# Hybrid decoder block: x loaded as rows, scaled and turned by TensorE, in place of x^T with sums over partitions

## The chip, the cores and the metric

One core of a Trainium2 chip runs the whole block as one launch. The metric is the device time in microseconds; three runs of the kernel before gave 1325.47, 1326.5 and 1329.25, median 1326.5. The engines named below are TensorE (PE; PEld is its weight load), VectorE (DVE), ScalarE (ACT), GpSimd (POOL) and the sync engine (SP), which issues nearly all loads.

## The reference

x is 1024 tokens by 1024 features, all float32. What the change touches is the first line of the block and the first product behind it:

```python
mod = silu(c) @ w_ada + b_ada            # six rows of 1024: shift_mix, scale_mix, gate_mix, ...
y   = x * rsqrt(mean(x * x, axis=-1) + 1e-6) * g_mix
h   = y * (1 + scale_mix) + shift_mix
qkv = h @ w_in                           # 1024 x 3072: q, k, v of 8 dilated and 8 stick-breaking heads
```

Then come the dilated ALiBi attention and the stick-breaking attention (64 wide heads), their RMS norms, the output projection with a gated residual, a second modulated RMS norm, a router (best of 4 groups, best 2 of its 8 experts), 32 SwiGLU experts of width 512, and a final RMS norm.

## The kernel before

**Layout.** The projection keeps features on the partitions: `hh[k]` and `hl[k]` (k = 0 to 7) are the high and the low part of h^T, each 128 features by 1024 tokens. A product in float32 is made of three passes in the faster float32r type: high weights by `hh`, low weights by `hh`, high weights by `hl`. For that the host hands x in two layouts: rows (`x`, used later for the residual) and turned (`xT`). All 128x1024 float32 tiles share one pool of 49 buffers (`slot`, L129), four PSUM banks are shared by `bank`, two double banks by `wide`.

**Loads.** SP issues them in program order: `c`, then `xT` as 16 pieces of 128x512 (first all eight k of tokens 0 to 511, then of 512 to 1023; L195 to L197), `cols` (biases and gains), `ident`, and the 20 loads of `LOADS0` (L51), 512 KB each: `10` is the 128x1024 block of w_ada^T that gives scale_mix for k = 0, `00` the one for shift_mix, `w0` and `w1` the weights of q and k of the first head pair, `w2` and `w3` those of v.

**The head (L249 to L312).** For each half of the tokens, ScalarE squares eight 128x512 tiles and VectorE adds them up (`add_sq`). The sum over the partitions is made by TensorE, four matmuls with a column of ones (`sums`); an inverse root by Newton steps (`rsqrt`, 12 small instructions for four columns on VectorE) gives 1/rms per token as a column, on GpSimd for the first half. `over_rows` brings it along the free axis: ident scaled by the roots, then a matmul with ones, so that PSUM holds 1/rms of each token on all partitions (`Rps`), copied to `Rb`. `w0_split(i)` makes the high part of a weight tile on ScalarE and the low part on the engine that `LO` names.

**The loop over k (L1074 to L1117).** `mod_k(k)` (L241) makes the gain `amix` and the shift of feature block k: two 128x1024 multiply-and-reduce instructions on VectorE (`ada_red`, L208, its line is L209) and two small ones. k = 0 is done in halves from `Rps` directly. For k from 1, GpSimd (VectorE for k = 1) multiplies `xT[k]` by `Rb`; ScalarE makes `hh[k] = gain * xT + shift` (L1093), ScalarE or VectorE makes the same in float32 (`tmp`), and VectorE takes the difference `hl[k]` (L1099, L1103). Each k then feeds 12 matmuls of 512 columns (L1119 to L1121, q and k of the first pair) and 15 of 256 columns (`v_first`, L1065, five of the eight token tiles). After the loop 72 matmuls of 256 columns make the other three token tiles. Each engine takes its instructions in program order, so a wait holds all behind it.

**Behind it.** The results are split into high and low parts, and the attention starts (L513 is its first VectorE step). All later stages are queued behind the earlier ones on each engine; the loads of the expert weights (L982) are tied to ScalarE instructions of the stage in which they are issued and to free buffers.

Of the kernel before, what the change touches and what calls it, by code (L numbers as in the profile page):

```python
# [7 lines left out]
F32 = mybir.dt.float32  # L8
# [4 lines left out]
AF = mybir.ActivationFunctionType  # L13
ALU = mybir.AluOpType
# [5 lines left out]
D = 1024  # L20
KT = 8
# [20 lines left out]
LDS = [6, 6, 11, 14, 18, 22, 28, 33, 33, 34]  # L42
PACE = 14
TZ, DZ = 2, 3
W2 = [0, 0]
W3 = [2, 3]
SK = 7
WT = 8
TM = "VVAAAAAA"
P2 = 2  # L50
LOADS0 = "10 w0 00 w1 11 01 w2 12 02 13 03 w3 14 04 15 05 16 06 17 07"  # L51
LO = 'GGGV'
M1 = "V"
VP = 5
VE = 'AVVAAVVV'
UT = 1
# [39 lines left out]
def build(nc, tc, I, out, cap=CAP):  # L96
# [6 lines left out]
    cp = pool("const", 1)  # L103
# [7 lines left out]
    E_ = dict(S=nc.sync, A=A, G=G, V=V)  # L111
# [26 lines left out]
    def f32(ap):  # L138
        return ap.bitcast(F32)
# [51 lines left out]
    crow = slot("crow")  # L191
    nc.sync.dma_start(crow[0:1], I["c"])
    halves = (slice(0, 512), slice(512, 1024))
    xT = [slot(f"xT{k}") for k in range(KT)]
    for c in halves:  # L195
        for k in range(KT):
            nc.sync.dma_start(xT[k][:, c], I["xT"][k * 128:(k + 1) * 128, c])  # L197
    nc.sync.dma_start(cols, I["cols"])
    nc.sync.dma_start(ident, I["ident"])
    sc = slot("sc")  # L200
# [7 lines left out]
    def ada_red(w, v, k):  # L208
        V.tensor_tensor_reduce(w, w, sc, op0=ALU.mult, op1=ALU.add, scale=1.0, scalar=0.0,  # L209
                               accum_out=modc[:, v * 8 + k:v * 8 + k + 1])  # L210
# [17 lines left out]
            v, k = int(o[0]), int(o[1])  # L228
            wa[v, k] = ada(v, k)

    def gain(k):
        ada_red(wa[1, k], 1, k)
        V.tensor_add(mod3[:, 1, k:k + 1], mod3[:, 1, k:k + 1], bad3[:, 1, k:k + 1])
        V.scalar_tensor_tensor(amix[:, k:k + 1], modc[:, 8 + k:9 + k], 1.0, g_mix[:, k:k + 1],
                               op0=ALU.add, op1=ALU.mult)

    def shift(k):
        ada_red(wa[0, k], 0, k)
        V.tensor_add(mod3[:, 0, k:k + 1], mod3[:, 0, k:k + 1], bad3[:, 0, k:k + 1])

    def mod_k(k):  # L241
        ada_red(wa[1, k], 1, k)
        ada_red(wa[0, k], 0, k)
# [6 lines left out]
    for c in halves:  # L250
        PE.matmul(cps[:, c], ones[0:1, :], crow[0:1, c], start=True, stop=True)
    A.activation(sc[:, 0:1], eps, AF.Silu)
    sq = [slot(f"xsq{k}") for k in range(KT)]
    rx = cp.tile([128, KT], F32, name="rx")
    dgs = slot("dgs")
    Rps = {}
    def warm(n):

        if n:
            scr = bank("scr")  # L260
            for _ in range(n * 4):
                PE.matmul(scr[:, 0:128], onesb, onesb, start=True, stop=True)

    def add_sq(h, ks):
        c = halves[h]
        for k in ks:
            A.activation(sq[k][:, c], xT[k][:, c], AF.Square)
            if k:
                V.tensor_add(sq[0][:, c], sq[0][:, c], sq[k][:, c])

    def sums(h):
        ssx = bank(f"ssx{h}", (128, 4))
        for tt in range(4):
            j = 4 * h + tt
            PE.matmul(ssx[:, tt:tt + 1], sq[0][:, j * 128:(j + 1) * 128], ones[:, 0:1], start=True, stop=True)
        warm(W2[h])
        return ssx

    def over_rows(h, eng):
        Rps[h] = bank(f"Rps{h}")  # L280
        for tt in range(4 * h, 4 * h + 4):
            dg = dgs[:, tt * 128:(tt + 1) * 128]
            if eng is A or tt % 2:
                A.activation(dg, ident, AF.Copy, scale=rx[:, tt:tt + 1])
            else:
                V.tensor_scalar_mul(dg, ident, rx[:, tt:tt + 1])
            PE.matmul(Rps[h][:, (tt - 4 * h) * 128:(tt - 4 * h + 1) * 128], ones, dg, start=True, stop=True)
        warm(W3[h])

    add_sq(0, range(KT))  # L290
    ss0 = cp.tile([128, 4], F32, name="ss0")
    ps = sums(0)
    add_sq(1, range(SK))
    A.activation(ss0, ps, AF.Copy)
    rsqrt(rx[:, 0:4], ss0, 4, 1.0 / D, G)
    add_sq(1, range(SK, KT))
    A.activation(sc, cps, AF.Silu)
    ss1 = sums(1)
    over_rows(0, A)
    wsp = {}  # L300

    def w0_split(i):
# [2 lines left out]
        E_[LO[i]].tensor_sub(lo, wraw[i], f32(hi))  # L305
        wsp[i] = [w.rearrange("p (k c) -> p k c", k=KT if i < 2 else 4) for w in (hi, lo)]

    Rb = slot("Rb")
    gain(0)
    w0_split(0)  # L310
    rsqrt(rx[:, 4:8], ss1, 4, 1.0 / D)
    over_rows(1, V)  # L312

    hh, hl = [], []
    pw = [wide("pj0"), wide("pj1")]
# [758 lines left out]
    for k in range(KT):  # L1074
        a = slot(f"hh{k}", F32R)
        b = slot(f"hl{k}", F32R)
        am, sh = amix[:, k:k + 1], modc[:, k:k + 1]
        if k == 0:
            c0, c1 = halves
            V.scalar_tensor_tensor(xT[k][:, c0], xT[k][:, c0], am, Rps[0], op0=ALU.mult, op1=ALU.mult)  # L1080
            shift(0)
            w0_split(1)
            V.scalar_tensor_tensor(xT[k][:, c1], xT[k][:, c1], am, Rps[1], op0=ALU.mult, op1=ALU.mult)
            for c in halves:
                A.activation(a[:, c], xT[k][:, c], AF.Identity, bias=sh)
            for c in halves:
                V.scalar_tensor_tensor(b[:, c], xT[k][:, c], sh, f32(a[:, c]), op0=ALU.add, op1=ALU.subtract)
            for h, c in enumerate(halves):
                A.activation(Rb[:, c], Rps[h], AF.Copy)
        else:  # L1090
            tmp = slot(f"tmp{k}")
            (E_[M1] if k == 1 else G).tensor_mul(xT[k], xT[k], Rb)
            A.activation(a, xT[k], AF.Identity, scale=am, bias=sh)  # L1093
            if TM[k] == "A":
                A.activation(tmp, xT[k], AF.Identity, scale=am, bias=sh)
            else:
                V.tensor_scalar(tmp, xT[k], am, sh, op0=ALU.mult, op1=ALU.add)
        if k and k < P2:
            V.tensor_sub(b, tmp, f32(a))  # L1099
        if k + 1 < KT:  # L1100
            mod_k(k + 1)
        if k and k >= P2:
            V.tensor_sub(b, tmp, f32(a))  # L1103
        if k in (0, 2):
            w0_split(2 + k // 2)
        if k == 4:
            seq[0][1]()
            seq[1][1]()
            load_bias(0)
# [12 lines left out]
        for tt in range(VP):
            v_first(k, tt)
# [428 lines left out]
def layout(x, c, w_ada, b_ada, g_mix, w_in, g_dil_out, g_sb_out, w_out, g_ffn,  # L1552
# [23 lines left out]
                         w_down[0].reshape(NE, 4, 128, 1024).transpose(0, 2, 1, 3).reshape(NE, 128, 4096)],  # L1576
                        axis=2)
    wr = np.concatenate([w_expert[0], w_group[0]], axis=1).reshape(8, 128, 36).transpose(1, 0, 2)
    arrays = dict(x=xr, xT=cc(xr.T), c=cc(c.reshape(1, 1024)), w_adaT=cc(w_ada[0].T), cols=cols,
                  wqk=cc(wqk), wv=cc(wv), w_out=cc(w_out[0]), wr=cc(wr), we=cc(we))  # L1580
    arrays.update(constants())
    return arrays
# [14 lines left out]
```

## Time and profile before

| | |
|---|---|
| median of 3 runs | 1326.5 us |
| profiled execution | 1328.25 us, of which the span 1326.5 |
| TensorE matmul / weight load busy | 1168.2 us (88%) / 686.3 (52%) |
| VectorE busy | 738.0 us (56%) |
| ScalarE busy | 530.5 us (40%) |
| GpSimd busy | 227.1 us (17%) |
| HBM | 278.56 MB read, 29.63 MB written |

Busy shares are means over stages: the first 100 us are the head and the first projection, then come the attention blocks, from about 740 us on the experts, whose weights are most of the bytes. The change lies in the first 100 us, so that stretch is read by itself.

### The profile page before, as it was taken

How to read it: one execution, taken by the hardware profiler on the slowest of the kernel's cores; microseconds unless marked ns; L12 is line 12 of the kernel's file. 1: busy time of each engine (PE TensorE's matmuls, PEld its weight loads, DVE VectorE, ACT ScalarE, POOL GpSimd, SP SyncE). 2: the span in 40 equal slices, each digit the busy share in tenths (PEclk: the TensorE clock that was granted, in tenths of full speed). 3: DMA queues.
4: the chain of work that ended last, by engine and by line, in shares of the span. 5: the costliest groups of instructions: out<-in, count | busy, mean ns of one | idle time of the engine just before them, and what ended most of it. 6: DMA issues, size and time to landing. Idle time of an engine off the chain costs nothing.

```text
span 1326.5 us, 19360 instructions
## 1 busy us (share of the span) xinstructions
PE 1168.2 (88%) x6810; PEld 686.3 (52%) x6810; DVE 738.0 (56%) x1433; ACT 530.5 (40%) x1080; POOL 227.1 (17%) x275
## 2 busy tenths in 40 slices
PE   4699989999999999699887999899999998888872
PEld 3497778778866887487666422223233322222220
DVE  6958773865497848968866243333333333323225
ACT  5346553666555445434634432232222222222312
POOL 3600010110100002222323111111111111111200
PEclk9799999999999999899999899999999999999986
DMA  9423442431001010356767899999999999999984
GB/s 350 169 69 97 153 159 90 149 60 69 24 25 48 17 64 1 126 208 225 250 219 273 303 318 367 339 387 373 370 375 375 370 371 369 368 386 379 387 332 175
DMA packets 89432, 304.80 MB, mean 230 GB/s; under 512 B 12402, under 2 KB 14834, under 8 KB 89330
## 3 DMA queue, kind: packets, MB, share of 16 engines
q1 hardware_dynamic: 81778, 282.00, 57.7%
q0 software_dynamic: 6400, 17.31, 5.3%
q10 hardware_dynamic: 1152, 4.19, 0.8%
q8 instruction: 56, 0.92, 0.3%
q14 instruction: 46, 0.38, 0.1%
HBM read 278.56 MB, written 29.63 MB: 232 GB/s over the span
## 4 chain that ended last, share of the span: by engine, by line
PE 43%; DMA 23%; DVE 22%; ACT 7%; issue 4%; POOL 1%; SPq 0%; POOLq 0%; DVEq 0%; ACTq 0%
DMA ew<-we 21%; PE gu L1270 5%; PE y L1270 4%; PE o L572 4%; DVE K L531 3%; DVE wada L209 2%; PE tp L548 2%; PE op L665 2%; PE op L667 2%; PE op L666 2%; DMA wada<-w_adaT 2%; PE y L1277 2%; DVE P L513 2%; PE pv L459 2%; PE pv L460 2%
## 5 line engine op out<-in xcount | busy, mean ns | idle before, releaser
L1270 PE MATMUL gu<-ew,xs 128*64 128x512 f32 x1024 | 251.6, 610 | 13.3 <-DMA ew<-we 9.8
L1329 DVE TENSOR_TENSOR ys<-y,bc_gate 64x512 f32<-64x512 f32 x60 | 41.3, 688 | 208.5 <-PE y L1277 120.8
L1270 PEld LDWEIGHTS gu<-ew,xs 128*64 128x64 f32 x1024 | 62.8, 136 | 147.3 <-issue 68.6
L1270 PE MATMUL y<-ew,at 128*64 128x512 f32 x512 | 124.5, 618 | 11.2 <-DMA ew<-we 10.0
L1247 ACT ACTIVATE xs<-xp,modc,affn 128x96 f32<-128x96 f32 (+1 forms) x128 | 51.6, 418 | 148.8 <-PE xp L1259 76.4
L548 PE MATMUL tp<-ident,P 128*128 128x128 f32 x576 | 89.0, 280 | 19.4 <-DVE P L532 9.6
L1342 POOL DMA_INDIRECT acc<-ys,lsP x26 | 37.2, 1433 | 369.4 <-DVE ys L1335 255.4
L531 DVE TENSOR_TENSOR_SCAN K<-K 128x1024 f32<-128x1024 f32 (+7 forms) x64 | 92.8, 1451 | 5.9 <-ACT K L519 5.7
L515 ACT ACTIVATE P<-P,st 128x1024 f32<-128x1024 f32 (+7 forms) x64 | 49.8, 778 | 90.2 <-DVE st L513 45.7
L548 PEld LDWEIGHTS tp<-ident,P 128*128 128x128 f32 x576 | 65.8, 141 | 38.1 <-issue 9.7
L1270 PEld LDWEIGHTS y<-ew,at 128*64 128x64 f32 x512 | 36.3, 142 | 95.1 <-issue 48.0
L572 PE MATMUL o<-PT,v 128*64 128x256 f32 (+1 forms) x640 | 75.1, 375 | 9.4 <-DVE PT L553 5.7
L1245 DVE TENSOR_SCALAR xs<-xp,affn,modc 128x96 f32<-128x96 f32 (+1 forms) x128 | 45.4, 362 | 59.0 <-ACT xs L1247 58.4
L519 ACT ACTIVATE K<-S 128x1024 f32<-128x1024 f32 (+7 forms) x64 | 41.8, 653 | 73.4 <-PE S L502 34.4
L1277 PE MATMUL gu<-ew,xs 128*32 128x512 f32 x576 | 70.9, 611 | 0.0
L209 DVE CUSTOM_DVE_ANT_0 wada<-wada,sc 128x1024 f32<-128x1024 f32 x48 | 64.4, 1353 | 9.6 <-DMA wada<-w_adaT 9.5
L513 DVE CUSTOM_DVE_ANT_0 P<-S,B 128x1024 f32<-128x1024 f32 (+7 forms) x64 | 48.2, 755 | 35.9 <-PE S L500 31.4
L1282 ACT ACTIVATE yt<-y 64x512 f32<-64x512 f32 x18 | 10.7, 593 | 143.1 <-PE xp L1259 111.9
L572 PEld LDWEIGHTS o<-PT,v 128*64 128x64 f32 x640 | 45.6, 141 | 39.5 <-DVE PT L553 8.2
L551 ACT ACTIVATE PT<-tp 128x512 f32<-128x512 f32 (+3 forms) x120 | 56.1, 495 | 14.8 <-PE tp L548 14.0
L532 DVE TENSOR_TENSOR P<-P,K 128x1023 f32<-128x1023 f32 (+7 forms) x64 | 51.5, 805 | 5.7 <-ACT P L520 0.8
L553 DVE COPY PT<-tp 128x512 f32<-128x512 f32 (+3 forms) x72 | 37.3, 536 | 17.8 <-PE tp L548 17.4
(641 smaller groups left out, 2507.3 us busy)
## 6 DMA issues: line engine op xcount, KB each, us to landing
ew<-we SPq DMA_DIRECT2D x384, 512.0 KB, 10.8
wada<-w_adaT SPq DMA_DIRECT2D x48, 512.0 KB, 5.7
wqk<-wqk SPq DMA_DIRECT2D x16, 512.0 KB, 3.9
xT<-xT SPq DMA_DIRECT2D x16, 256.0 KB, 5.3
wv<-wv SPq DMA_DIRECT2D x8, 512.0 KB, 7.6
B<-bias SPq DMA_DIRECT2D x8, 512.0 KB, 5.4
wo<-w_out SPq DMA_DIRECT2D x8, 512.0 KB, 5.0
x<-x SPq DMA_DIRECT2D x8, 512.0 KB, 4.2
```

Of the source, the lines that this page charges most:

```text
L209: V.tensor_tensor_reduce(w, w, sc, op0=ALU.mult, op1=ALU.add, scale=1.0, scalar=0.0, accum_out=modc[:, v * 8 + k:v * 8 + k + 1])
L513: V.tensor_tensor_reduce(e, s, Bt[p, hd][:, :L], op0=ALU.add, op1=ALU.min, scale=-0.125, scalar=BIG, accum_out=st[:, 0:1])
L515: A.activation(e, e, AF.Exp, bias=st[:, 0:1], scale=-1.0, accum_out=st[:, 2:3])
L531: V.tensor_tensor_scan(k[:, :L], k[:, :L], k[:, :L], 1.0, op0=ALU.mult, op1=ALU.bypass)
L532: V.tensor_mul(b[:, 1:L], b[:, 1:L], k[:, 0:L - 1])
L548: PE.transpose(tp[:, jl - 4 * x, :], e[:, (jl - qo) * 128:(jl - qo) * 128 + 128], ident)
L551: A.activation(dst, tp[:, j0 - 4 * x:j1 - 4 * x, :], AF.Copy)
L572: PE.matmul(ps[hd * 64:hd * 64 + 64, 0:w], VV[p][:, j, hd * 64:hd * 64 + 64], pt[hd][jl // 4][:, jl % 4, 0:w], start=(n == 0), stop=(n == ...
L1245: V.tensor_scalar(dst, src, affn[:, k:k + 1], modc[:, 24 + k:25 + k], op0=ALU.mult, op1=ALU.add)
L1247: A.activation(dst, src, AF.Identity, scale=affn[:, k:k + 1], bias=modc[:, 24 + k:25 + k])
L1270: PE.matmul(ps[h * 64:h * 64 + 64, 0:512], a[:, i, 0:64], w[:, h * 512:h * 512 + 512], start=(i == 0), stop=(i == n - 1))
L1277: PE.matmul(ps[r:r + 32, 512:1024], a[:, j, 64:96], w[:, h * 512:h * 512 + 512], start=(j < 2), stop=(j >= n - 2))
```

## The change

x is loaded as eight tiles of 128 tokens by 1024 features (`xn`), `xT` is no longer an input. Each row's squares are summed along it by the instruction that squares (ScalarE for six tiles, VectorE for tiles 1 and 3); the inverse roots of four tiles at a time, both on VectorE, scale the rows in place; TensorE turns them, four 128x128 transposes into a PSUM bank, and ScalarE (once VectorE) copies a bank to `xT[k]`. The loop over k keeps one path for all k: `hh`, `tmp` on ScalarE, `hl` on VectorE, with no multiplication by `Rb`. All low parts of the first weights go to VectorE.

```diff
@@ -42,15 +42,10 @@
 LDS = [6, 6, 11, 14, 18, 22, 28, 33, 33, 34]
 PACE = 14
 TZ, DZ = 2, 3
-W2 = [0, 0]
-W3 = [2, 3]
-SK = 7
 WT = 8
-TM = "VVAAAAAA"
-P2 = 2
 LOADS0 = "10 w0 00 w1 11 01 w2 12 02 13 03 w3 14 04 15 05 16 06 17 07"
-LO = 'GGGV'
-M1 = "V"
+LO = 'VVVV'
+W3 = 3
 VP = 5
 VE = 'AVVAAVVV'
 UT = 1
@@ -191,10 +186,9 @@
     crow = slot("crow")
     nc.sync.dma_start(crow[0:1], I["c"])
     halves = (slice(0, 512), slice(512, 1024))
-    xT = [slot(f"xT{k}") for k in range(KT)]
-    for c in halves:
-        for k in range(KT):
-            nc.sync.dma_start(xT[k][:, c], I["xT"][k * 128:(k + 1) * 128, c])
+    xn = [slot(f"xn{t}") for t in range(KT)]
+    for t in range(KT):
+        nc.sync.dma_start(xn[t], I["x"][t * 128:(t + 1) * 128, :])
     nc.sync.dma_start(cols, I["cols"])
     nc.sync.dma_start(ident, I["ident"])
     sc = slot("sc")
@@ -228,16 +222,6 @@
             v, k = int(o[0]), int(o[1])
             wa[v, k] = ada(v, k)
 
-    def gain(k):
-        ada_red(wa[1, k], 1, k)
-        V.tensor_add(mod3[:, 1, k:k + 1], mod3[:, 1, k:k + 1], bad3[:, 1, k:k + 1])
-        V.scalar_tensor_tensor(amix[:, k:k + 1], modc[:, 8 + k:9 + k], 1.0, g_mix[:, k:k + 1],
-                               op0=ALU.add, op1=ALU.mult)
-
-    def shift(k):
-        ada_red(wa[0, k], 0, k)
-        V.tensor_add(mod3[:, 0, k:k + 1], mod3[:, 0, k:k + 1], bad3[:, 0, k:k + 1])
-
     def mod_k(k):
         ada_red(wa[1, k], 1, k)
         ada_red(wa[0, k], 0, k)
@@ -250,10 +234,9 @@
     for c in halves:
         PE.matmul(cps[:, c], ones[0:1, :], crow[0:1, c], start=True, stop=True)
     A.activation(sc[:, 0:1], eps, AF.Silu)
-    sq = [slot(f"xsq{k}") for k in range(KT)]
+    xT = [slot(f"xT{k}") for k in range(KT)]
     rx = cp.tile([128, KT], F32, name="rx")
-    dgs = slot("dgs")
-    Rps = {}
+    ssx = cp.tile([128, KT], F32, name="ssx")
     def warm(n):
 
         if n:
@@ -261,42 +244,25 @@
             for _ in range(n * 4):
                 PE.matmul(scr[:, 0:128], onesb, onesb, start=True, stop=True)
 
-    def add_sq(h, ks):
-        c = halves[h]
-        for k in ks:
-            A.activation(sq[k][:, c], xT[k][:, c], AF.Square)
-            if k:
-                V.tensor_add(sq[0][:, c], sq[0][:, c], sq[k][:, c])
-
-    def sums(h):
-        ssx = bank(f"ssx{h}", (128, 4))
-        for tt in range(4):
-            j = 4 * h + tt
-            PE.matmul(ssx[:, tt:tt + 1], sq[0][:, j * 128:(j + 1) * 128], ones[:, 0:1], start=True, stop=True)
-        warm(W2[h])
-        return ssx
-
-    def over_rows(h, eng):
-        Rps[h] = bank(f"Rps{h}")
-        for tt in range(4 * h, 4 * h + 4):
-            dg = dgs[:, tt * 128:(tt + 1) * 128]
-            if eng is A or tt % 2:
-                A.activation(dg, ident, AF.Copy, scale=rx[:, tt:tt + 1])
-            else:
-                V.tensor_scalar_mul(dg, ident, rx[:, tt:tt + 1])
-            PE.matmul(Rps[h][:, (tt - 4 * h) * 128:(tt - 4 * h + 1) * 128], ones, dg, start=True, stop=True)
-        warm(W3[h])
-
-    add_sq(0, range(KT))
-    ss0 = cp.tile([128, 4], F32, name="ss0")
-    ps = sums(0)
-    add_sq(1, range(SK))
-    A.activation(ss0, ps, AF.Copy)
-    rsqrt(rx[:, 0:4], ss0, 4, 1.0 / D, G)
-    add_sq(1, range(SK, KT))
-    A.activation(sc, cps, AF.Silu)
-    ss1 = sums(1)
-    over_rows(0, A)
+    def square(t, eng):
+        if eng is A:
+            A.activation(xT[t], xn[t], AF.Square, accum_out=ssx[:, t:t + 1])
+        else:
+            V.tensor_tensor_reduce(xT[t], xn[t], xn[t], op0=ALU.mult, op1=ALU.add, scale=1.0, scalar=0.0,
+                                   accum_out=ssx[:, t:t + 1])
+
+    def roots(h):
+        rsqrt(rx[:, 4 * h:4 * h + 4], ssx[:, 4 * h:4 * h + 4], 4, 1.0 / D)
+
+    def norm_row(t):
+        V.tensor_scalar(xn[t], xn[t], rx[:, t:t + 1], None, op0=ALU.mult)
+
+    def turn(h, k, eng):
+        tp = bank(f"xt{h}_{k}")
+        for t in range(4):
+            PE.transpose(tp[:, t * 128:(t + 1) * 128], xn[4 * h + t][:, k * 128:(k + 1) * 128], ident)
+        (A.copy if eng is A else eng.tensor_copy)(xT[k][:, halves[h]], tp)
+
     wsp = {}
 
     def w0_split(i):
@@ -305,11 +271,25 @@
         E_[LO[i]].tensor_sub(lo, wraw[i], f32(hi))
         wsp[i] = [w.rearrange("p (k c) -> p k c", k=KT if i < 2 else 4) for w in (hi, lo)]
 
-    Rb = slot("Rb")
-    gain(0)
+    for t in range(KT):
+        square(t, V if t in (1, 3) else A)
+        if t == 3:
+            roots(0)
+    A.activation(sc, cps, AF.Silu)
+    for t in range(4):
+        norm_row(t)
+    roots(1)
+    for k in range(KT):
+        turn(0, k, A)
+    for t in range(4, KT):
+        norm_row(t)
+    mod_k(0)
     w0_split(0)
-    rsqrt(rx[:, 4:8], ss1, 4, 1.0 / D)
-    over_rows(1, V)
+    for k in range(KT):
+        turn(1, k, A if k != 1 else V)
+        if k == 1:
+            w0_split(1)
+    warm(W3)
 
     hh, hl = [], []
     pw = [wide("pj0"), wide("pj1")]
@@ -1075,32 +1055,12 @@
         a = slot(f"hh{k}", F32R)
         b = slot(f"hl{k}", F32R)
         am, sh = amix[:, k:k + 1], modc[:, k:k + 1]
-        if k == 0:
-            c0, c1 = halves
-            V.scalar_tensor_tensor(xT[k][:, c0], xT[k][:, c0], am, Rps[0], op0=ALU.mult, op1=ALU.mult)
-            shift(0)
-            w0_split(1)
-            V.scalar_tensor_tensor(xT[k][:, c1], xT[k][:, c1], am, Rps[1], op0=ALU.mult, op1=ALU.mult)
-            for c in halves:
-                A.activation(a[:, c], xT[k][:, c], AF.Identity, bias=sh)
-            for c in halves:
-                V.scalar_tensor_tensor(b[:, c], xT[k][:, c], sh, f32(a[:, c]), op0=ALU.add, op1=ALU.subtract)
-            for h, c in enumerate(halves):
-                A.activation(Rb[:, c], Rps[h], AF.Copy)
-        else:
-            tmp = slot(f"tmp{k}")
-            (E_[M1] if k == 1 else G).tensor_mul(xT[k], xT[k], Rb)
-            A.activation(a, xT[k], AF.Identity, scale=am, bias=sh)
-            if TM[k] == "A":
-                A.activation(tmp, xT[k], AF.Identity, scale=am, bias=sh)
-            else:
-                V.tensor_scalar(tmp, xT[k], am, sh, op0=ALU.mult, op1=ALU.add)
-        if k and k < P2:
-            V.tensor_sub(b, tmp, f32(a))
+        tmp = slot(f"tmp{k}")
+        A.activation(a, xT[k], AF.Identity, scale=am, bias=sh)
+        A.activation(tmp, xT[k], AF.Identity, scale=am, bias=sh)
         if k + 1 < KT:
             mod_k(k + 1)
-        if k and k >= P2:
-            V.tensor_sub(b, tmp, f32(a))
+        V.tensor_sub(b, tmp, f32(a))
         if k in (0, 2):
             w0_split(2 + k // 2)
         if k == 4:
@@ -1576,7 +1536,7 @@
                          w_down[0].reshape(NE, 4, 128, 1024).transpose(0, 2, 1, 3).reshape(NE, 128, 4096)],
                         axis=2)
     wr = np.concatenate([w_expert[0], w_group[0]], axis=1).reshape(8, 128, 36).transpose(1, 0, 2)
-    arrays = dict(x=xr, xT=cc(xr.T), c=cc(c.reshape(1, 1024)), w_adaT=cc(w_ada[0].T), cols=cols,
+    arrays = dict(x=xr, c=cc(c.reshape(1, 1024)), w_adaT=cc(w_ada[0].T), cols=cols,
                   wqk=cc(wqk), wv=cc(wv), w_out=cc(w_out[0]), wr=cc(wr), we=cc(we))
     arrays.update(constants())
     return arrays
```

## Rows read from the trace of the kernel before

**Rows 1.** Stretches: length, busy us per engine (instructions), granted clock, DMA share, GB/s.
```profile
0.00:31.40 31.40, 12.53 (x56) 9.52 (x57) 19.48 (x38) 17.04 (x30) 11.69 (x29) 0.98 0.93 346
31.40:59.80 28.40, 15.51 (x57) 11.47 (x57) 28.05 (x25) 7.54 (x9) 21.96 (x9) 0.74 0.54 219
59.80:97.60 37.80, 37.80 (x233) 34.37 (x234) 23.36 (x41) 18.71 (x23) 1.91 (x2) 0.94 0.20 60
```

**Rows 2.** Chain of waits, 40 to 104 us: start, length, what.
```profile
46.84 3.31 DVE wada L209
...
58.50 1.23 DVE hl L1103
59.77 0.79 PE pj L1121
```

**Rows 3.** GpSimd in order of time: start, length, line, operation, shapes.
```profile
37.27 18.41 POOL L1092 TENSOR_TENSOR xT<-xT,Rb 128x1024 f32<-128x1024 f32 x6
```

**Rows 4.** VectorE in order of time, 42 to 140 us.
```profile
64.58 1.22 DVE L209 CUSTOM_DVE_ANT_0 wada<-wada,sc 128x1024 f32<-128x1024 f32 x1
...
67.26 1.22 DVE L1103 TENSOR_TENSOR hl<-tmp,hh 128x1024 fp32r<-128x1024 f32 x1
...
105.00 0.75 DVE L529 TENSOR_SCALAR P<-P,st 128x1024 f32<-128x1024 f32 x1
```

**Rows 5.** TensorE in order of time: the first projection matmul to the next weights.
```profile
31.40 0.80 PE L1119 MATMUL pj<-hh,w_0h 128*128 128x512 f32 x1 [3.25 <-ACT hh L1085]
...
70.68 0.40 PE L1119 MATMUL pj<-hh,w_0h 128*128 128x512 f32 x1
...
75.22 0.40 PE L1119 MATMUL pj<-hh,w_0h 128*128 128x512 f32 x1
...
88.84 0.28 PE L1069 MATMUL pj<-w_2h,hh 128*128 128x256 f32 x1
...
97.48 0.40 PE L416 MATMUL pj<-hh,w01h 128*128 128x512 f32 x1
```

**Rows 6.** Stretches cut where the granted clock changed.
```profile
30.40:37.20 6.80, 5.70 (x13) 4.04 (x13) 6.63 (x9) 3.29 (x5) 3.38 (x2) 0.50 1.02 419
...
64.50:97.60 33.10, 33.10 (x223) 30.64 (x223) 18.73 (x34) 16.06 (x21) 1.91 (x2) 1.00 0.21 65
```

**Rows 7.** ScalarE in order of time: the last square.
```profile
15.94 0.63 ACT L267 ACTIVATE xsq<-xT 128x512 f32<-128x512 f32 x1
```

**Rows 8.** Stretch of the 512 KB loads behind x.
```profile
17.50:45.00 27.50, 15.30 (x73) 12.66 (x73) 23.96 (x35) 8.29 (x14) 20.77 (x24) 0.86 1.02 415
```

**Rows 9.** Line L1364: ns shortest/median/longest, first and last start.
```profile
L1364 ACT ACTIVATE fy<-fx x8: 1039/1044/1049, 1292.3 to 1306.2; 128x1024 f32<-128x1024 f32 x8
L1364 ACT ACTIVATION_READ_ACCUMULATOR fy<-fx x8: 185/190/193, 1293.2 to 1307.1; 128x1 f32 x8
```

**Rows 10.** VectorE in order of time: first and last of 12 for the roots.
```profile
20.20 0.16 DVE L171 TENSOR_SCALAR rs<-ssx 128x4 f32<-128x4 f32 x1 [0.43 <-PE ssx L275]
...
22.25 0.16 DVE L183 SCALAR_TENSOR_TENSOR rx<-rs 128x4 f32<-128x4 f32 x1
```

**Rows 11.** TensorE in order of time: eight transposes of the attention.
```profile
105.97 1.03 PE L548 MATMUL tp<-ident,P 128*128 128x128 f32 x8
```

**Rows 12.** Line L548, all its transposes: ns shortest/median/longest.
```profile
L548 PE MATMUL tp<-ident,P x576: 270/273/473, 106.0 to 693.0; 128*128 128x128 f32 x192
```

**Rows 13.** ScalarE by shape, 100 to 400 us: busy us, mean ns, idle before.
```profile
L551 ACT ACTIVATE PT<-tp 128x512 f32<-128x512 f32 x44 | 25.2, 592 | 2.6 <-PE tp L548 2.3
```

**Rows 14.** ScalarE by shape, 0 to 100 us.
```profile
L1093 ACT ACTIVATE hh<-xT,modc,amix 128x1024 fp32r<-128x1024 f32 x7 | 8.7, 1242 | 26.3 <-POOL tid L1151 13.9 <-DVE xT L1092 6.9 <-DVE amix L245 5.4
```

**Rows 15.** Stretches behind the projection, as in rows 1.
```profile
104.00:612.00 508.00, 475.80 (x2956) 382.43 (x2955) 368.25 (x614) 263.26 (x549) 73.12 (x72) 0.98 0.27 88
...
800.00:1200.00 400.00, 367.00 (x2042) 112.04 (x2040) 139.27 (x257) 111.39 (x206) 57.87 (x48) 0.99 1.02 371
```

**Rows 16.** Waits of the issue queue, 0 to 100 us: total, times, longest.
```profile
SPq L117 <- PE pj L1120: 12.0, 1, 12.0
```

## The prediction

> **What bounds the kernel now.** I read the stretches first, then the chain of waits, then TensorE's instructions in order of time. The stretches [rows 1] cut the head of the span at the first projection matmul (31.40) and at the point where TensorE stops waiting (59.80). Up to 31.40 the work is the sums over x. From 31.40 to 59.80 VectorE is busy 28.05 of 28.40 us and TensorE 15.51; from 59.80 to 97.60 TensorE is busy for all 37.80 us. The chain [rows 2] says the same: up to 58.50 it runs on VectorE (ada reductions, then the difference that makes `hl`), from 59.77 on it is matmuls. So the projection is fed by VectorE for its first third and is TensorE's own time afterwards.
>
> Why VectorE is slow there: while GpSimd multiplies xT by Rb, six times in 18.41 us [rows 3], an ada reduction takes 3.31 us [rows 2]; once GpSimd is done, the same instruction takes 1.22 [rows 4].
>
> What the projection costs TensorE by itself [rows 5]: one k takes 75.22 - 70.68 = 4.54 us at the full clock, and the 72 last matmuls 97.48 - 88.84 = 8.64. Eight k and the tail make 36.3 + 8.6 = 45.0 us. It began at 31.40 and ended at 97.48, 66.1 us: 21 us go to waiting and to the lower clock. From 30.40 to 37.20 the granted clock was 0.50, the 1.2 GHz level, with TensorE busy 5.70; over the last 33.10 us it was 1.00 [rows 6].
>
> **The change, part by part.** I follow the four engines to the first moment at which TensorE has work without a gap (`hl` of k = 0), then let TensorE run.
>
> *Loads.* The 4.19 MB of x come as 8 transfers of 512 KB in place of 16 of 256 KB; the issue queue is passed eight instructions sooner by `cols`, `ident` and the ada and weight loads behind it. The transfers were full anyway (share 0.93 [rows 1]), so little is won. Bounds for x all landed: before, its last square began at 15.94 [rows 7]; at the 415 GB/s of the later loads with 4 KB rows [rows 8], 4.19 MB from 2.5 us on end at 12.6. I take 14.5.
>
> *Squares and roots.* Six of the eight squares run on ScalarE with the sum taken along the row. The same form costs 1.04 us and 0.19 for reading the sum at the end of the kernel [rows 9], less than a tile of 512 KB takes to land (1.26 us at 415 GB/s), so only the last one counts: 14.5 + 1.25 = 15.75. The Silu that makes `sc` follows, a pass of the same size, 1.04: 16.8. The chain for four inverse roots is 12 small VectorE instructions from 20.20 to 22.41, 2.2 us [rows 10]. The first chain and four scalings (0.75 each, the 128x1024 scaling at 105.00 [rows 4]) need rows 0 to 3 only and are done by about 15.7.
>
> *Removed.* 16 half squares, 14 adds, the 16 sum matmuls, the diagonals and the matmuls that spread the roots, both root chains at their old places, GpSimd's six multiplications (18.41 us [rows 3]) and its three differences of weights. GpSimd had none of the later work of this stage, so nothing moves up behind it but memsets and two iotas.
>
> *First half of the transposes.* TensorE turns 32 tiles. At the full clock eight follow each other in 1.03 us [rows 11], one alone takes 0.27 [rows 12], so they start (1.03 - 0.27) / 7 = 0.109 apart, 0.43 for four; at the half clock 0.87. ScalarE copies each bank of four in 0.59 [rows 13]. Bounds: 16.8 + 8 x 0.59 = 21.5 if ScalarE sets the pace, 15.75 + 8 x 0.87 + 0.6 = 23.3 if TensorE stays at 1.2 GHz. I take 22.3, near the middle, since nothing dense precedes them.
>
> *VectorE beside it.* Second chain of roots 15.75 to 17.95; four scalings 3.0: 20.95; the gain and shift of k = 0: 67.26 - 64.58 = 2.68 [rows 4]: 23.6; the low part of w0 1.2: 24.8; one copy from PSUM, at most 0.75: 25.6; the low part of w1: 26.8; gain and shift of k = 1: 29.5.
>
> *ScalarE's second half.* High part of w0, a copy, high part of w1, six copies: 2 x 1.1 + 7 x 0.59 = 6.3, to 28.6; the twelve warm-up matmuls lie under it. Then `hh` of k = 0, 1.24 [rows 14]: 29.85, where the first two matmuls start (31.40 before); `tmp` to 31.0; VectorE, free since 29.5, makes `hl` in 1.22 [rows 4]: 32.2. TensorE is thus dense from 32.2. The head gains nothing: rows first, transposes after, come to the same half microsecond as sums and spread roots.
>
> *The loop over k.* Per k VectorE needs gain and shift of the next k and one difference, 2.68 + 1.22 = 3.9 us [rows 4], against TensorE's 4.54; with GpSimd silent there is no reason for more. The low parts of w2, w3 and of the next weights add 1.2 each after k = 0, 2 and 6. `hl` of k = 1 is due at 32.2 + 1.2 + 3.9 = 37.3, of k = 3 at 32.2 + 2 x 1.2 + 3 x 3.9 = 46.3, of k = 7 (no gain and shift behind it) at 60.4. ScalarE needs 2 x 1.24 per k. TensorE, with k = 0 at the low clock as before, loses half of a stretch like [rows 6]: 3 us. It finishes k = 0 at 32.2 + 4.08 (two matmuls of 0.23 are already done) + 3.0 = 39.3 and needs `hl` of k = 1 at 39.8, of k = 3 at 48.8, of k = 7 at 67. All are there, by 2.5 us at the tightest. So it runs through: 39.3 + 7 x 4.54 + 8.64 = 79.7, against 97.48.
>
> **The sum**: 97.48 - 79.7 = 17.8 us earlier for all that hangs on the projection. The profiled execution took 1328.25 (span 1326.5 and 1.75 around it), which would become 1310.4; it lay 1.75 above the median of 1326.5, so the median should be 1308.7. Ends: x at 12.6, copies at ScalarE's pace and no low clock give dense work at 29.5 and an end at 74.0, plus 1 us of waiting for `hl`: 22.5 won. x at 15.9, all transposes slow (2.4) and a second low stretch (3) give 86.5: 11 won.
>
> **A rule weighed against the trace.** The trace has no stretch of transposes alone: those of [rows 11] follow matmuls at the full clock. The Trainium skill, "TensorE: Matmul & The Clock Gate", section "Part 4: PE-mode transpose", states that the full clock does not engage for transposes. By it the third rival below holds; no run here shows it yet.
>
> **Rivals.**
> 1. *The gain does not reach the end.* The weights of the experts fill the DMA engines from 800 to 1200 us (share 1.02 [rows 15]); if their start were set by something that the front does not move, 1326.5 stays. Against it: from 104 to 612 us the share is 0.27 and TensorE is busy 475.80 of 508.00 [rows 15], so the stretch behind the projection starts when the projection ends, and the expert loads are queued behind ScalarE's work of the last attention block. Nothing in the program waits for a time of day.
> 2. *Slower: TensorE is held at 1.2 GHz through the projection.* The place is the k loop: if each k again left a gap, the clock would fall back as it did before 59.80 (mean 0.74 [rows 1]). At half clock the 44.5 us after 32.2 take up to 89: end 121, 23.7 late, 1350. It decides from the point at which low stretches exceed 6 us by 2 x 17.8 = 36 us. Against it: 33.10 of 33.10 us busy at 1.00 once the feed was faster than TensorE [rows 6], and the feed is 3.9 against 4.54.
> 3. *Transposes leave the clock low.* Then TensorE paces both halves: half 0 ends at 23.3 in place of 22.3, and the six last copies come up to 0.87 apart in place of 0.59, 1.7 more, of which four filled banks save a part: together 2.4 later at most; k = 0 is slow as already counted. End 82.1, 15.4 won: 1311.1.
> 4. *A load late for want of a buffer.* All large tiles share 49 buffers, and the front now holds eight rows and eight turned tiles at once. The issue queue waited 12.0 us for a buffer that a matmul held [rows 16], and everything behind it waits too. If such a wait fell on an ada load of the loop, 12.0 less the 2.5 of slack costs 9.5: 1318. Against it: the eight rows come free by 28, and the eight square tiles, one diagonal tile and Rb are gone.
>
> **Chances.** Forecast 0.62, rival 3 0.18, rival 4 0.09, rival 1 0.05, rival 2 0.04; 0.02 for more than 22.5 won. A measurement of this kernel can tell about 0.3%, 4 us, from no change. Faster takes the forecast, 3, 4 and the rest: 0.91; same is rival 1: 0.05; slower is rival 2: 0.04. The range takes in both ends of the sum, 1304 to 1315.5, widened to 1303 to 1317 for the scatter of the runs and part of rival 4.
>
> **What would show it.** GpSimd without 128x1024 work before 100 us. Ada reductions of 1.22 us throughout. First projection matmul near 30, dense matmuls from 32, one low-clock stretch at most after that, `hl` differences about 3.9 apart, the first next-weight matmul (L416 before) near 80, the first bias step of the attention near 84.5 in place of 102.26. From there on the same distances as before. Wrong if TensorE waits for `hl` or `hh` after k = 1, if the first projection matmul comes after 34, or if the stretch from the first attention step to the end changes by more than 3 us.

## The result and the profile after

| | before | after |
|---|---|---|
| median | 1325.99 us (4 runs, 1323.27 to 1329.25) | 1306.15 us (4 runs, 1297.16 to 1309.85) |
| profiled execution, its span | 1328.25, 1326.5 | 1308.14, 1306.4 |
| first projection matmul | 31.40 | 27.55 |
| first matmul of the next weights (the next heads' q and k) | 97.48 | 77.28 |
| first bias step of the attention (`P<-S,B`, VectorE) | 102.26 | 82.00 |
| from there to the end of the span | 1224.2 | 1224.4 |

The ratio after to before is 0.9851, interval 0.9822 to 0.988: faster by 1.5%, 2.5 us under the forecast of 1308.7. The bias step (the expectations below call it the first attention step), before and then after:

```profile
102.26 1.22 DVE L513 CUSTOM_DVE_ANT_0 P<-S,B 128x1024 f32<-128x1024 f32 x1
```
```profile
82.00 1.23 DVE L493 CUSTOM_DVE_ANT_0 P<-S,B 128x1024 f32<-128x1024 f32 x1
```

It comes 20.26 us earlier and the distance behind it is the same to 0.2 us, so in these two profiles all of the gain lies in the first 82 us. That the two distances agree so closely is luck: in the profiles of the experiments the distance runs from 1214.1 (e4) to 1227.0 (e1).

The totals scatter more than the front does. The four runs of after have spans of 1308.0, 1306.4, 1302.4 and 1295.4 at mean granted clocks of 0.961, 0.963, 0.965 and 0.972. In what follows the start of that bias step is therefore the sharper reading, and the time says only roughly whether it arrives.

Stretches of the kernel after, columns as in [rows 1], cut at the first matmul of the dense run (29.94), at the end of k = 0 (36.87) and at the next weights (77.28):

```profile
0.00:29.94 29.94, 15.20 (x82) 11.15 (x82) 20.90 (x53) 22.45 (x36) 1.23 (x14) 0.99 0.95 375
29.94:36.87 6.93, 6.93 (x26) 5.96 (x27) 6.86 (x11) 4.96 (x5) 0.00 (x0) 0.57 1.03 416
36.87:77.28 40.41, 40.41 (x263) 36.97 (x262) 25.18 (x46) 19.50 (x24) 1.89 (x2) 1.00 0.36 130
...
104.00:612.00 508.00, 478.49 (x2975) 384.34 (x2971) 364.79 (x608) 258.10 (x541) 72.25 (x80) 0.98 0.29 97
800.00:1200.00 400.00, 368.65 (x2038) 112.70 (x2040) 138.43 (x256) 110.92 (x206) 57.86 (x48) 0.99 1.02 374
```

Against [rows 1]: TensorE was idle for 12.89 us of the stretch from 31.40 to 59.80. Now it is busy for every one of the 47.34 us from 29.94 to 77.28. GpSimd, the fifth figure, does nothing at all in k = 0 and two memsets behind it. The last two rows stand beside [rows 15]: the attention and the experts are as they were.

VectorE of the kernel after in order of time (start, length, line, operation, shapes), the rows that answer to [rows 2] and [rows 4]:

```profile
30.94 1.22 DVE L203 CUSTOM_DVE_ANT_0 wada<-wada,sc 128x1024 f32<-128x1024 f32 x1
...
33.62 1.22 DVE L1063 TENSOR_TENSOR hl<-tmp,hh 128x1024 fp32r<-128x1024 f32 x1
...
37.44 1.22 DVE L1063 TENSOR_TENSOR hl<-tmp,hh 128x1024 fp32r<-128x1024 f32 x1
```

An ada reduction takes 1.22 us at a place where one took 3.31, and the differences follow each other in 3.82. TensorE in order of time, beside [rows 5]; the bracket is its idle time and what ended it:

```profile
27.55 0.50 PE L1079 MATMUL pj<-hh,w_0h 128*128 128x512 f32 x1 [1.37 <-ACT hh L1059]
...
29.94 0.79 PE L1081 MATMUL pj<-hl,w_0h 128*128 128x512 f32 x1 [1.65 <-DVE hl L1063]
...
36.87 0.40 PE L1079 MATMUL pj<-hh,w_0h 128*128 128x512 f32 x1
...
77.28 0.40 PE L396 MATMUL pj<-hh,w01h 128*128 128x512 f32 x1
```

No wait comes after 29.94. Before, the first matmul with `hl` came at 32.42:

```profile
32.42 0.63 PE L1121 MATMUL pj<-hl,w_0h 128*128 128x512 f32 x1
```

So the 20.2 us of the next weights (97.48 to 77.28) split into about 2.5 from an earlier start and 17.7 from the run itself. Of these 17.7, 12.9 are waits that are gone. The other 4.8 are the same matmuls at a higher clock (TensorE busy for 47.34 us now, 52.2 before): before, the granted clock was 0.50 not only around k = 0 but also from 44.1 to 50.8 and from 57.7 to 64.5.

### The profile page after: what moved, and what is told of

It reads as the page before. It is cut to its first block, busy times and chain, and to the rows that moved or that the text cites. A ratio compares the mean times of both kernels' runs of the same rounds, so it can differ in the third digit from the quotient of the medians.

```text
span 1306.4 us, 19380 instructions
## 1 busy us (share of the span) xinstructions
PE 1167.7 (89%) x6834; PEld 688.1 (53%) x6834; DVE 720.4 (55%) x1439; ACT 534.7 (41%) x1083; POOL 193.4 (15%) x251
## 4 chain that ended last, share of the span: by engine, by line
PE 44%; DMA 28%; DVE 18%; ACT 6%; issue 3%; POOL 0%; SPq 0%; POOLq 0%; DVEq 0%; ACTq 0%
DMA ew<-we 24%; PE o L552 4%; PE gu L1230 4%; PE y L1230 4%; DVE K L511 3%; PE tp L528 3%; PE op L645 2%; PE op L647 2%; PE op L646 2%; PE pj L396 2%; PE pj L397 2%; PE pj L398 2%; DMA wada<-w_adaT 2%; PE pv L439 2%; PE pv L441 2%
## 5 line engine op out<-in xcount | busy, mean ns | idle before, releaser
L495 ACT ACTIVATE P<-P,st 128x1024 f32<-128x1024 f32 (+7 forms) x64 | 49.8, 778 | 92.3 <-DVE st L508 47.0
L203 DVE CUSTOM_DVE_ANT_0 wada<-wada,sc 128x1024 f32<-128x1024 f32 x48 | 58.7, 1236 | 10.2 <-DMA wada<-w_adaT 10.1
L1256 DVE TENSOR_TENSOR act<-sg,gu 64x512 f32<-64x512 f32 x32 | 22.1, 690 | 44.4 <-ACT sg L1255 35.1
```

The lines of the kernel that those rows point to most:

```text
L495: A.activation(e, e, AF.Exp, bias=st[:, 0:1], scale=-1.0, accum_out=st[:, 2:3])
```

## The experiments

| run | first bias step | median | before, beside it | ratio, interval |
|---|---|---|---|---|
| e1_gpsimd_products | 92.3 | 1319.64 | 1321.51 | 0.997, 0.9951 to 0.999 |
| e2_before_no_product | 87.5 | 1309.71 | 1321.51 | 0.9905, 0.9877 to 0.9933 |
| e3_before_product_on_vector | 94.6 | 1316.41 | 1321.51 | 0.995, 0.993 to 0.997 |
| e4_warm_17 | 81.3 | 1300.58 | 1321.51 | 0.9849, 0.9818 to 0.988 |
| e5_after_again | 82.5 | 1303.55 | 1324.64 | 0.9841, 0.9815 to 0.9868 |
| e6_first_k_early | 80.7 | 1303.06 | 1324.64 | 0.9854, 0.9829 to 0.9878 |
| e7_gpsimd_memsets | 86.7 | 1307.6 | 1324.64 | 0.9885, 0.9858 to 0.9913 |
| e8_head_longer | 84.7 | 1307.78 | 1324.64 | 0.9883, 0.9857 to 0.9909 |
| e9_gpsimd_memsets_in_loop | 81.1 | 1303.84 | 1322.99 | 0.9868, 0.9808 to 0.9928 |
| e10_low_parts_on_gpsimd | 82.6 | 1307.94 | 1322.99 | 0.9881, 0.9853 to 0.991 |

Theory A is the prediction's: GpSimd's products made VectorE slow, VectorE starved TensorE, and the low clock came with the gaps. The rivals say that the head, the number of instructions per k, or the clock by itself made the difference.

**e1: the products put back, with nobody to read them.**

```diff
+    junk = slot("junk")
     for k in range(KT):
         ...
+        if 0 < k < 7:
+            G.tensor_mul(junk, xT[k], sc)
```

> The kernel after, with six GpSimd products of 128x1024 float32 put back into the k loop (k = 1 to 6), written to a tile that nobody reads; no instruction waits for them. Theory A (the gain comes from VectorE no longer being slowed by GpSimd in the k loop): the products take about 3 us each, beginning when xT[1] is turned near 24 us, and until about 43 us the reductions and differences on VectorE take 2.2 to 3.4 us in place of 1.22. Before, the 18.4 us of products cost VectorE some 12 us; so hl of k = 1 comes at 41 to 46 in place of 34.8, the first attention step at 90 to 96 in place of 82.0, and the time is 1314 to 1320. Theory B (the gain comes from what the loop waits for, the product itself, or from a shorter head): nothing waits for these products, so the first attention step stays at 82 and the time at about 1306.

GpSimd, VectorE and TensorE's waits (line, releaser, total us, times, longest) of this run:

```profile
24.87 18.80 POOL L1061 TENSOR_TENSOR junk<-xT,sc 128x1024 f32<-128x1024 f32 x6 [23.40 <-DVE xT L264]
```
```profile
25.76 3.37 DVE L203 CUSTOM_DVE_ANT_0 wada<-wada,sc 128x1024 f32<-128x1024 f32 x1
...
34.75 3.39 DVE L1066 TENSOR_TENSOR hl<-tmp,hh 128x1024 fp32r<-128x1024 f32 x1
...
44.68 1.21 DVE L203 CUSTOM_DVE_ANT_0 wada<-wada,sc 128x1024 f32<-128x1024 f32 x1
```
```profile
PE pj L1084 <- DVE hl L1066: 11.5, 2, 9.4
```

The products take 18.80 us (18.41 in [rows 3]), VectorE takes 3.4 us for what takes 1.2 as soon as they end, and TensorE waits 9.4 us for the first `hl`. The bias step comes at 92.3, inside A's 90 to 96. So a product that feeds nothing takes back half of the gain: that half is contention alone, with no change in what the loop waits for. In time 16 to 17 us come back (ratio 0.997 against 0.9851 and 0.9841 for after), more than the 10 at the bias step; the rest falls behind it, and its cause stays open.

**e2 and e3: the kernel before without the product, and with it on VectorE.** Both also make all `tmp` on ScalarE and all low parts on VectorE, as after does. e2 leaves the product by `Rb` out, so the rows of k = 1 to 7 stay unscaled.

```diff
-TM = "VVAAAAAA"
-LO = 'GGGV'
+TM = "AAAAAAAA"
+LO = 'VVVV'
...
-            (E_[M1] if k == 1 else G).tensor_mul(xT[k], xT[k], Rb)
+            V.tensor_mul(xT[k], xT[k], Rb)          # e3; in e2 the line is left out
```

> The kernel before, with the product of xT and the spread roots left out for k from 1 (that part of the norm is then missing for those k), all float32 copies on ScalarE and all low parts of the first weights on VectorE: the k loop of the kernel after behind the head of the kernel before, with no rows and no transposes. Theory A (loop): the ada reductions take 1.22 us throughout, hl comes every 3.9 us, TensorE runs without a gap from about 39 us, the first attention step is at 85 to 88 in place of 102.26, and the time near 1310 to 1312. Theory B (the head with rows is what gains): the first attention step stays above 98 and the time above 1320.

> The kernel before with the product moved from GpSimd to VectorE for all k from 1, all float32 copies on ScalarE, all low parts of the first weights on VectorE: still x^T and spread roots. VectorE then needs 3.9 + 1.2 = 5.1 us per k, more than TensorE's 4.54. Theory A: no instruction of VectorE is slowed, hl comes every 5.1 us, TensorE waits about half a microsecond per k, the first attention step at 87 to 91, the time 1311 to 1316: most of the gain without rows. Theory B (rows and transposes are needed for the gain): first attention step above 95, time above 1318.

e2 met A (87.5 in 85 to 88); e3 missed it (94.6, not 87 to 91) and stayed just under the rival's 95; its time, 1316.41, lies between the two as well. VectorE of e3, product and difference of three k:

```profile
44.99 1.22 DVE L1092 TENSOR_TENSOR xT<-xT,Rb 128x1024 f32<-128x1024 f32 x1
...
48.82 1.22 DVE L1103 TENSOR_TENSOR hl<-tmp,hh 128x1024 fp32r<-128x1024 f32 x1
...
54.91 1.22 DVE L1103 TENSOR_TENSOR hl<-tmp,hh 128x1024 fp32r<-128x1024 f32 x1
...
59.86 1.22 DVE L1103 TENSOR_TENSOR hl<-tmp,hh 128x1024 fp32r<-128x1024 f32 x1
```

Nothing is slow here, yet the differences come 4.95 us apart (6.09 with a low part between), more than TensorE's 4.54: VectorE is the bound. For k = 1 and 7 it also waits 2.4 and 2.5 us for its own product to come back through ScalarE as `tmp`. These two, and no slow instruction, put it at 94.6. The two runs split the gain at the bias step: 102.26 to 94.6 for taking the product and the three low parts off GpSimd (with the two `tmp` moved to ScalarE; the parts of this step are not told apart), to 87.5 for having no product, to 82.0 for the rows. Of the last 5.5, k = 0 ends 2.7 earlier (39.56 against 36.87) and the run behind it is 2.8 shorter, since e2 still waits, 1.8 of it for `hl`.

**e4: 68 warm-up matmuls in place of 12.**

```diff
-W3 = 3
+W3 = 17
```

> The kernel after with 68 small warm-up matmuls ahead of the projection in place of 12, which fill TensorE's idle time from 25.4 to 29.2 us. In the kernel after the granted clock fell to 0.50 at 29.9 and k = 0 took 6.9 us in place of 4.1. Theory A (TensorE's idle time ahead of the projection is what lets the clock fall): the clock stays at 1.00, k = 0 is done at about 34, TensorE waits about 0.4 us for hl of k = 1, the first attention step comes at 79 to 80 in place of 82.0, the time is about 2.5 us below the kernel after, near 1303.5. Rival (the clock falls whatever is run there, or VectorE's feed is the bound from k = 1): first attention step at 81.5 to 82.5, time as after.

TensorE around them, and the stretch in which the clock was low (columns as in [rows 1]):

```profile
24.44 2.43 PE L263 MATMUL xt<-ident,xn 128*128 128x128 f32 x12 [0.78 <-ACT xT L264]
26.66 5.08 PE L245 MATMUL scr<-onesb 128*128 128x128 bf16 x68
31.55 0.48 PE L1079 MATMUL pj<-hh,w_0h 128*128 128x512 f32 x1
...
36.19 0.40 PE L1079 MATMUL pj<-hh,w_0h 128*128 128x512 f32 x1
```
```profile
25.40:28.80 3.40, 3.40 (x29) 3.34 (x29) 3.34 (x6) 2.93 (x5) 0.00 (x0) 0.53 1.02 417
```

k = 0 ran at full clock, as meant: all its matmuls took 4.64 us, where in after those from the first `hl` on alone took 6.93. But the low stretch had only moved ahead of it: it slowed the transposes and the warm-ups, and the latter held the first projection matmul until 31.55. The bias step came at 81.3, where I had written 79 to 80. The ratio is that of after.

**e5: after once more.**

> The kernel after, unchanged, as the measure for the run beside it. Every theory expects the first attention step at 81 to 83 us, and a ratio to the kernel before of 0.983 to 0.987.

82.5 and a ratio of 0.9841: the result repeats on another chip. k = 0 was at the low clock again.

**e6: k = 0 made ahead of most of the second half of the transposes.**

```diff
-    for k in range(KT):
-        turn(1, k, A if k != 1 else V)
-        if k == 1:
-            w0_split(1)
+    turn(1, 0, A)
+    first = [slot("hh0", F32R), slot("hl0", F32R), slot("tmp0")]
+    A.activation(first[0], xT[0], AF.Identity, scale=amix[:, 0:1], bias=modc[:, 0:1])
+    V.tensor_scalar(first[2], xT[0], amix[:, 0:1], modc[:, 0:1], op0=ALU.mult, op1=ALU.add)
+    V.tensor_sub(first[1], first[2], f32(first[0]))
+    turn(1, 1, V)
+    w0_split(1)
+    for k in range(2, KT):
+        turn(1, k, A)
...          (in the loop over k, these three steps are left out for k = 0)
```

> The kernel after with the work of k = 0 moved ahead of most of the second half of the transposes: hh of k = 0 on ScalarE right behind its own copy, its float32 copy on VectorE, and the difference at once. Theory A (TensorE's start of dense work is set by the order on ScalarE, 29.9 us after, and VectorE's feed of 3.8 us per k is the next bound): TensorE's projection starts dense near 26.5 with a wait of up to 2 us for the low part of w2, the first attention step comes at 79 to 80.5 in place of 82.0, the time 1.5 to 3 us below the kernel after, at the edge of what can be told. Rival (VectorE's feed sets the end already): first attention step at 81.5 to 82.5. If the earlier start leaves more gaps and the clock falls for longer, it comes later than 83.

TensorE of this run; the second row is the first projection matmul:

```profile
26.37 2.23 PE L263 MATMUL xt<-ident,xn 128*128 128x128 f32 x12 [2.03 <-ACT xT L264]
...
29.64 0.78 PE L1084 MATMUL pj<-hh,w_0h 128*128 128x512 f32 x1
```

`hl` of k = 0 is made early (from 25.24), but TensorE takes its work in order and waits 2.0 us for a bank in the middle of the transposes, so the dense run starts at 29.64 in place of 29.94, not near 26.5 as I had written. The bias step is the earliest of all with 80.7, just behind the 79 to 80.5 I expected, but mostly for another reason: the low stretch came earlier (27.7 to 31.1, more than half of it on the transposes and warm-ups), and k = 0 was done at 34.93 in place of 36.87. In time nothing can be told from after.

**e7 and e9: GpSimd busy with memsets, which read nothing.** e9 ties them to the loop by a one-column copy.

```diff
+    junk = slot("junk")
     for k in range(KT):
         ...
+        if 0 < k < 7:
+            G.tensor_copy(junk[:, 0:1], xT[k][:, 1023:1024])    # e9 alone
+            for _ in range(3):
+                G.memset(junk, 0.0)
```

> The kernel after with 18 GpSimd memsets of 128x1024 float32 in the k loop, some 18 us of GpSimd time that only writes, to a tile that nobody reads, in place of the six products of the earlier experiment. If GpSimd slows VectorE's two-input instructions by reading SBUF beside them, the reductions and differences stay at 1.22 us, the first attention step at 82 to 83 and the time as the kernel after. If any GpSimd work does it, as the six products did, the first attention step comes at 90 to 93 and the time is 8 to 12 us longer.

> As the experiment with 18 memsets, but each group of three now follows a copy of one column of xT[k] by GpSimd, so that it can't start before xT[k] is turned and all of it falls into the k loop (from about 24 to 43 us), none into the head. Theory A (in the k loop GpSimd hurts by reading SBUF beside VectorE's two-input instructions; writes alone do not): reductions and differences stay at 1.22 us, the first attention step at 82 to 83.5. Rival (any GpSimd work of that length does it, as the products did, 92.3): 90 or later.

e7's memsets waited for nothing, so they ran from 1.41 to 21.2, in the head, and left the question of the loop unanswered. They hit something else. VectorE of e7:

```profile
8.87 1.23 DVE L251 CUSTOM_DVE_ANT_0 xT<-xn 128x1024 f32<-128x1024 f32 x1 [1.63 <-DMA xn<-x]
...
13.27 5.06 DVE L258 TENSOR_SCALAR xn<-xn,rx 128x1024 f32<-128x1024 f32 x4
```

Four scalings, one input each, take 5.06 us in place of 2.74 in after; the square with its sum, two inputs, stays at 1.23. Some one-input steps of the roots, 128x4 only, take 0.91 to 0.99 in place of 0.16 or 0.17. Together they put the second four scalings 5.0 us later (22.06 against 17.06 in after) and the bias step at 86.7, 4.2 to 4.7 later than in after. In e9 the memsets lie where the products lay. GpSimd, then VectorE:

```profile
25.49 2.97 POOL L1063 MEMSET junk<- 128x1024 f32 x3
```
```profile
31.32 1.22 DVE L203 CUSTOM_DVE_ANT_0 wada<-wada,sc 128x1024 f32<-128x1024 f32 x1
...
34.00 1.22 DVE L1068 TENSOR_TENSOR hl<-tmp,hh 128x1024 fp32r<-128x1024 f32 x1
```

1.22 throughout, and the bias step at 81.1, a little ahead of the 82 to 83.5 expected: the low clock lasted only from 30.1 to 33.5, and k = 0 took 5.66 us in place of 6.93. GpSimd's being busy costs the loop nothing; what it reads does. The Trainium skill, "SBUF — State Buffer", section "Who interferes with whom", says as much: a VectorE instruction with two inputs in SBUF contends with a GpSimd instruction that reads SBUF, not with one that only writes, while a scaling can contend with GpSimd when it runs in a two-port mode. e1 (3.4 us) and e9 (1.22) agree on the first; e7 fits the second, though no run shows in which mode its scalings ran.

**e8: the head made longer on ScalarE.**

```diff
+    extra = slot("extra")
+    for _ in range(4):
+        A.activation(extra, xn[7], AF.Square)
     A.activation(sc, cps, AF.Silu)
```

> The kernel after with four more ScalarE squares of 128x1024 (into a tile nobody reads) between the last square and the Silu, so that the head takes 3.8 to 4.2 us longer and nothing else changes. If a microsecond of the head is a microsecond of the whole (the pass-through on which the sum rests), the first attention step comes at 85.8 to 86.3 in place of 82.0, and the time is 4 us longer than the kernel after, a ratio to before near 0.988. If VectorE's feed or a later stage absorbs it, the first attention step moves by less than 2 us, or the distance from there to the end shrinks by as much.

ScalarE's four squares, then TensorE at the start of the dense run and of k = 1:

```profile
14.97 4.31 ACT L280 ACTIVATE extra<-xn 128x1024 f32<-128x1024 f32 x4
```
```profile
33.78 0.50 PE L1084 MATMUL pj<-hl,w_0h 128*128 128x512 f32 x1 [1.66 <-DVE hl L1066]
...
39.55 0.40 PE L1082 MATMUL pj<-hh,w_0h 128*128 128x512 f32 x1
```

4.31 us of work move the dense run by 3.84, so ScalarE's queue sets the head's end. The bias step moves by 2.2 to 2.7 only (84.7 against 82.5 and 82.0; I had written 85.8 to 86.3): k = 0 took 5.77 us in place of 6.93, since its matmuls were slow from 34.5 to 37.9 only. So the head's delay passes through, less what the clock gave back (3.84 - 1.16 = 2.7).

**e10: three low parts back on GpSimd.**

```diff
-LO = 'VVVV'
+LO = 'GGGV'
```

> The kernel after with the low parts of w0, w1 and w2 back on GpSimd, as before: the last part of the change by itself. Theory A (GpSimd's reads slow VectorE's two-input instructions): VectorE is spared 3 x 1.14 us and loses about 2.2 us at each of the four to five reductions and differences that run beside 3 x 2.4 to 3.3 us of GpSimd; hl of k = 1 comes 1 to 4 us later than 34.8 and the first attention step at 82.5 to 85.5. Rival (offloading three instructions of VectorE is a plain gain): the first attention step at 80 to 81.5.

GpSimd, then VectorE of this run:

```profile
31.33 2.64 POOL L271 TENSOR_TENSOR w_2l<-wv,w_2h 128x1024 fp32r<-128x1024 f32 x1 [3.07 <-ACT w_2h L270]
```
```profile
31.61 3.44 DVE L203 CUSTOM_DVE_ANT_0 wada<-wada,sc 128x1024 f32<-128x1024 f32 x1
...
36.52 1.22 DVE L1063 TENSOR_TENSOR hl<-tmp,hh 128x1024 fp32r<-128x1024 f32 x1
```

One difference on GpSimd holds one reduction on VectorE for 3.44 us: a pass of 1.2 us moved to the idle engine costs VectorE 2.2. `hl` of k = 1 is 2.9 us later than in after (33.62), and TensorE, which waits for it nowhere in after, waits here. TensorE in order of time, the last row being the wait:

```profile
31.75 0.50 PE L1081 MATMUL pj<-hl,w_0h 128*128 128x512 f32 x1 [1.78 <-DVE hl L1063]
...
35.96 0.40 PE L1079 MATMUL pj<-hh,w_0h 128*128 128x512 f32 x1
...
37.79 0.50 PE L1081 MATMUL pj<-hl,w_0h 128*128 128x512 f32 x1 [1.20 <-DVE hl L1063]
```

The dense run starts 1.8 us later and waits 1.2 more. That the bias step is still at 82.6 comes from k = 0, which ran at full clock here (4.21 us for 6.93): A's delay is shown at `hl`, but its price at the bias step is mixed with the clock's. There is no low stretch at all in this part of the run, though the waits are as long as in after (columns as in [rows 1]):

```profile
20.30:91.80 71.50, 63.08 (x400) 55.02 (x399) 55.93 (x92) 43.95 (x58) 9.82 (x12) 1.00 0.49 187
```

## Why the prediction was right

*The loop.* Right, and nearly to the number. VectorE needs 3.82 us per k (3.9 predicted) against TensorE's 4.54; TensorE does not wait for `hl` again. From the end of k = 0 to the next weights it took 40.41 us, where 7 x 4.54 + 8.64 = 40.42. e1 and e9 show the reason: GpSimd's reads, put back alone, bring back 3.4 us per VectorE instruction; its writes don't.

*The low clock in k = 0.* The size was right: 6.93 us in place of 4.08, 2.85 lost, 3.0 predicted. That it would fall there was carried over from before ("at the low clock as before"), and it is not the rule. The clock fell at 29.1, after the gaps around the last transposes, but e8, e9, e4 and e10 show k = 0 with a part of a low stretch on it (5.77 and 5.66 us) or none (4.64 for all its matmuls, and 4.21), each time behind a later start. What makes it fall is not shown: e10 has waits of 1.20, 1.78 and 1.20 us there and stays at 1.00.

*The head.* Here the step failed that I put as "the head gains nothing": the first matmul came 2.3 us before its due time (27.55 for 29.85), and so did the dense run (29.94 for 32.2). ScalarE, which e8 shows to set it, in the kernel after:

```profile
13.71 1.06 ACT L249 ACTIVATE xT<-xn 128x1024 f32<-128x1024 f32 x1
...
19.01 2.06 ACT L264 COPY xT<-xt 128x512 f32<-128x512 f32 x4 [0.32 <-PE xt L263]
```

and the chain of waits (start, length, what) from there on:

```profile
21.07 0.96 ACT w_0h L270
22.03 0.47 ACT xT L264
22.50 0.96 ACT w_1h L270
23.45 2.12 ACT xT L264 x5
25.68 0.69 ACT xT L264
26.37 1.13 ACT hh L1059
27.50 1.14 ACT tmp L1060
28.66 1.24 DVE hl L1063
29.94 0.79 PE pj L1081
```

The last square with its sum was done at 14.85 in place of 15.75: 0.9. It started at 13.71 without a wait, so x had landed by then, where I had taken 14.5. Silu and the first half's copies were done at 21.07 in place of 22.3: 0.3 more. From there to `hh` it took 5.30 in place of 6.3: 1.0 more, and `hh` itself 0.1. Most of the last three is one mistake: I added up durations. Copies of 0.59 us each start 0.5 apart (four end 2.06 after the first starts), high parts of 1.10 start 0.96 apart, 1.24 is 1.13. A queue moves at the distance between starts.

*The sum.* The head's 2.3 us is nearly the whole error from there on. Next weights at 77.28 for 79.7, bias step at 82.00 for 84.5, median 1306.15 for 1308.7: the same 2.5 us each time. That the median agrees so closely is luck, with totals of after between 1297 and 1310.

*The rivals.* Rival 1 is out: the distance from the bias step to the end is 1224.4 (1224.2 before), and the ratio of e5 repeats the gain in time. Rival 2 is out: the clock is 1.00 from 36.87 to 77.28. Rival 4 priced a wait that exists but hurts nobody: SP waited up to 12.8 us for a buffer, yet neither VectorE, ScalarE nor TensorE waited for a load between 18 and 80 us.

Rival 3, transposes that leave the clock low, is out by the pace, though not at once. Three stretches of after in which TensorE does nothing but transposes (TensorE's busy time and count come first):

```profile
14.10:16.50 2.40, 2.33 (x10) 1.97 (x11) 2.16 (x12) 2.24 (x5) 0.00 (x0) 1.00 1.03 423
16.50:18.90 2.40, 2.40 (x13) 2.40 (x12) 2.30 (x6) 1.66 (x3) 0.00 (x0) 1.00 1.02 416
18.90:22.10 3.20, 3.12 (x29) 2.88 (x27) 3.19 (x6) 3.09 (x6) 0.00 (x0) 1.00 1.03 420
```

10, 13 and then 29 transposes: 0.24, 0.18 and 0.11 us each, the last at the full-clock step of 0.109 worked out from [rows 11]. The single starts are 0.21 us apart up to 18.7 and 0.11 from 18.9 on. The clock column is no help here: the trace has no record of the clock before 18.9, and the column reads 1.00 where there is none. e5 has 7, 14 and 29 in the same stretches. So the first 21 transposes went at about half the pace, and ScalarE waited 1.0 us for them in four copies; that is part of what I had allowed for by taking 22.3 and not 21.5. The sentence of the Trainium skill on which the rival stood ("TensorE: Matmul & The Clock Gate", section "Part 4: PE-mode transpose") does not hold for these transposes of 128x128 float32: the full pace came while TensorE ran nothing else.

## What to carry to other kernels

Before giving a pass to an idle GpSimd, look at what runs beside it: six products of 3.1 us that fed another engine made VectorE's two-input passes 2.8 times as long, and the engine they starved was a third one. A layout that removes the pass beats a better place for it (94.6 with the product on VectorE, 82.0 without). Sum a queue by the distance between starts, not by durations.

## What the runs showed of the hardware

- Beside a GpSimd product or difference that reads two 128x1024 tiles, a VectorE pass with two inputs takes 2.5 to 3.4 us in place of 1.22 (before, e1, e10); even one of 128x2 took 2.18 (e1). It looks like taking turns, one instruction each: 18.80 us of products hold six VectorE instructions (five of 128x1024 and that of 128x2). That is argued from the counts, not shown.
- GpSimd memsets leave those passes alone (1.22 in e9) and double VectorE's one-input scalings, 2.74 to 5.06 us for four (e7).
- Transposes by themselves brought TensorE from 0.21 to 0.11 us from start to start, at about 18.8 us in after.
- The low stretch of the clock ahead of or in k = 0 moves with small changes of the head: in k = 0 in after and e5, in the transposes and warm-ups in e4 (25.6 to 29.0), and none up to 91.8 in e10. What brings it and what fixes its length stay open.
